# Turning the gated FFN chunks with VectorE blocks and strided stores instead of TensorE transposes

## The chip, the core and the metric

The kernel runs on one core of a Trainium2 chip. The core has a matrix engine (TensorE, PE in the profile, with its weight loads as PEld), a vector engine (VectorE, DVE), a scalar engine (ScalarE, ACT), GpSimd (POOL) and a queue that issues DMA transfers (SyncE, SP). The engines run side by side, each with its own instructions in a fixed order, and wait for each other by semaphores. DMA transfers are moved by 16 DMA engines. The metric is the time of one execution on the device in microseconds.

## The reference: what is computed

One decoder layer on 512 tokens of width 2048, in float32. The part around the change is the last line, the gated feed-forward network (FFN) with 5632 hidden columns:

```python
mix = jnp.concatenate([out_a.astype(x.dtype), out_b.astype(x.dtype)], axis=-1)
x = x + mix @ w_out[l]
h2 = rms_norm(x, norm2_g[l])
x = x + (jax.nn.silu(h2 @ w_gate[l]) * (h2 @ w_up[l])) @ w_down[l]
```

Before it come the input projection, a gated linear attention on four heads and a dilated attention on eight heads, which the change does not touch.

## The kernel before

**Products.** A float32 product is made from single-pass products of rounded parts: an operand is split into a rounded high part and the rest. ACT makes the high part of a weight tile (`wh`, line 376) and DVE the low part (`wl`, line 380). On top of that the kernel multiplies matrices with Strassen's scheme in Winograd's form: each product of 2x2 blocks takes seven block products P1 to P7 in place of eight. For them DVE adds and subtracts weight tiles (line 298).

**Pairs and steps.** The work goes over "pairs" of 512 output columns. An FFN pair j (there are 11, 0 to 10) multiplies the normed tokens with 512 columns of `w_gate` and the same 512 of `w_up`. Its seven products take the order P1, P5, P6, P3, P7, P2, P4, each over four groups of rows: 28 steps of twelve 128x512 matmuls (line 405), eight with `wh` and four with `wl`. A step needs one `wh` and one `wl`; two buffers of each exist. The weight tiles of a pair are called a, b, d and c in the order in which they are loaded, four of each, 512 KB per tile, and twelve buffers hold them. P5 uses b - a, P7 d - b, P6 d - a and P4 c - a (`wa<-wb,wa` and so on at line 298).

**The gated chunk.** When both the gate and the up columns of a half of the tokens (256 of 512, two tiles `m` of 128) are done, `final_ffn` takes Silu on ACT and multiplies on DVE (line 1396). The result is a tile of 128 tokens by 512 hidden columns. The down projection needs it with the hidden columns on the partitions. So `transposed_store` (line 1092) turns it: eight 128x128 transposes on PE into two PSUM banks, two copies by ACT into the tiles `oT` and `PT` (line 1107), and two stores of 256 KB to DRAM (`p_d`, line 1116). The first half of a pair does this in the middle of step 26 of its pair, the second half in step 2 of the next pair.

**What reads it.** After the second half, `sums_job` loads four parts of the chunk (`r<-p_d`, line 1167), forms the sums S1 to S4 that the down projection will need on DVE (lines 1421 to 1428) and stores them (`S_d`, line 1416). During pair 10, `down_jobs` loads parts and sums for the first stage of the down projection and splits them (line 199).

**What sets the order.** The code of each step is written in one order, but a scheduler of the framework then places the instructions of each engine, and the DMA issues of SP, by its own estimate of when their inputs are there. Each engine and SP keep to the order so found: a waiting instruction holds up all behind it. The tile pool `mp` gives each of `oT` and `PT` one buffer, so a new tile waits until the store of the old one has landed. A DMA also waits until the eighth one before it has landed.

Of the kernel before, what the change touches and what calls it, by code (L numbers as in the profile page):

```python
# [18 lines left out]
P = 128  # L19
# [112 lines left out]
def block_kernel(ctx: ExitStack, tc: tile.TileContext, ins, out):  # L132
    nc = tc.nc
# [18 lines left out]
    def nm(s):  # L152
        uid[0] += 1
        return f"{s}_{uid[0]}"

    def dram(shape, name):
        return dr.tile(shape, F32, name=name, tag=name)

    def bank():
        return ps.tile([P, 512], F32, name=nm("bank"), tag="bank")  # L160

    def work(tag, shape=(P, 512), bufs=1):
        return mp.tile(list(shape), F32, name=nm(tag), tag=tag, bufs=bufs)
# [7 lines left out]
    store = nc.sync.dma_start  # L171
# [14 lines left out]
    done = set()  # L186


    class Operand:


        def __init__(self, groups):
            self.groups = groups
            self.t = {}
# [71 lines left out]
    def unfolded(t):  # L266

        return t.rearrange("p (a b) -> p b a", b=2)

    def halves(t):  # L270
        return t.rearrange("p (b a) -> p b a", b=2)
# [311 lines left out]
    def later(units, fn, hold=False):  # L583

        deferred.append([units, fn, hold])
# [506 lines left out]
    def transposed_store(tiles, half, dsts, gains=None, spare=None):  # L1092

        for b in range(2):
            bk = bank().rearrange("p (j n) -> p j n", j=2)
            for jj in range(2):
                for m in range(2):
                    f = (2 * b + jj) * P
                    nc.tensor.transpose(  # L1099
                        bk[:, jj, m * P : (m + 1) * P], tiles[m][:, f : f + P], ident  # L1100
                    )
            if spare is None:
                d = work(("oT", "PT")[b], (P, 2, 256))
            else:
                d = spare[b]
            if gains is None:
                nc.scalar.copy(d, bk)
            else:
                for jj in range(2):
                    nc.scalar.activation(  # L1110
                        d[:, jj, :], bk[:, jj, :], AF.Copy,
                        scale=gains[:, 2 * b + jj : 2 * b + jj + 1],
                    )
            if dsts is None:
                continue
            store(dsts[b][half], d)
            done.add((id(dsts[b]), half))
# [255 lines left out]


    rows_n = [(512, 0), (768, 256), (1536, 1024), (1792, 1280)]
    p_d = [dram([2, P, 2, 256], f"p_d{b}") for b in range(22)]
    tok_scale = lambda half, m: rs2[:, 2 * half + m : 2 * half + m + 1]

    def final_ffn(j):
        ups = {}  # L1380

        def final(half, which, tiles, acc_):
            if which == 1:
                ups[half] = tiles
                return
            up = ups[half]
            for m in range(2):
                if tiles is None:
                    s = work(("q", "k")[m])
                    nc.scalar.activation(  # L1390
                        halves(s), unfolded(acc_[m]), AF.Silu, scale=tok_scale(half, m)
                    )
                else:
                    s = tiles[m]
                    nc.scalar.activation(s, s, AF.Silu)
                nc.vector.tensor_tensor(up[m], up[m], s, op=ALU.mult)
            def rest():
                transposed_store(up, half, p_d[2 * j : 2 * j + 2])
                if half == 1:
                    background.append(sums_job(j))  # L1400

            later(1 + (half == 1), rest)

        return final
# [4 lines left out]
    def sums_job(j):  # L1409

        top, bot = p_d[2 * j], p_d[2 * j + 1]
        tt = nc.vector.tensor_tensor
        s, t, u, v = part(bot, 1)(), part(top, 1)(), part(top, 0)(), part(bot, 0)()

        def put(name, src):
            store(sums_d[j][name][0], src)
            done.add((id(sums_d[j][name]), 0))

        yield
        yield  # L1420
        tt(s, t, s, op=ALU.add)
        put("S1", s)
        tt(t, u, t, op=ALU.subtract)
        put("S3", t)
        yield
        tt(u, s, u, op=ALU.subtract)
        put("S2", u)
        tt(v, v, u, op=ALU.subtract)
        put("S4", v)
        yield  # L1430
# [139 lines left out]
```

## Time and profile before

| what | value |
|---|---|
| time of three runs, median (lowest to highest) | 1930.76 us (1928.1 to 1931.49) |
| the profiled execution | 1928.26 us, span 1926.5 us |
| PE busy | 1915.5 us, 99% of the span |
| DVE busy | 1648.5 us, 86% |
| ACT busy | 1091.1 us, 57% |
| 128x128 transposes on PE, all (line 1099) | 248 |
| DMA packets | 150360, of which 15494 under 512 bytes |

In this profile a line of a group names the source line, the engine and the operation, then the tiles written and read and their shapes; the time in order names start and duration in microseconds, and in brackets how long the engine was idle before and what released it. "Busy" of PE counts pipelined matmuls whose ends are modelled. SPq is the queue that issues DMAs; its durations are those of the issue, not of the transfer. The granted clock of PE is 1.000 throughout.

### The profile page before, as it was taken

The page shows a single profiled execution, that of the slowest core. Times are in us where ns is not written, and L with a number is a line of the kernel's source. Part 1 is how long each engine was busy: PE and PEld are TensorE (multiplying, and loading weights), DVE is VectorE, ACT ScalarE, POOL GpSimd, SP SyncE. Part 2 cuts the span into 40 slices and gives each one's busy share as a digit, 9 for nine tenths or more (in the row PEclk, how much of TensorE's full clock was granted, in tenths as well). Part 3 has the DMA queues.
Part 4 walks back from the last instruction along what each step waited for, and adds up shares of the span by engine and source line. Part 5 has one row for each costly group of instructions (what it writes and reads, how often), then busy time and mean ns, then how long its engine had stood idle before and what let it go on. Part 6 is the DMA issues. An engine that isn't in the chain of part 4 may idle for free.

```text
span 1926.5 us, 25570 instructions
## 1 busy us (share of the span) xinstructions
PE 1915.5 (99%) x9178; PEld 1662.2 (86%) x9178; DVE 1648.5 (86%) x1912; ACT 1091.1 (57%) x1611; POOL 13.4 (1%) x22
## 2 busy tenths in 40 slices
PE   9999999999999999999999999999999999999999
PEld 7888888888888888888888888888888888888887
DVE  8898797778899998887877878878879989989987
ACT  8654564567776675554544544544546646546443
POOL 0000010000000000000000000000000000000000
PEclk9999999999999999999999999999999999999999
DMA  9536445444537454354355354454455865855762
GB/s 339 207 111 248 152 160 186 137 164 142 195 112 260 155 187 154 136 181 162 129 180 164 132 175 156 140 186 139 157 183 177 279 217 182 294 194 181 242 218 66
DMA packets 150360, 345.75 MB, mean 179 GB/s; under 512 B 15494, under 2 KB 42671, under 8 KB 150232
## 3 DMA queue, kind: packets, MB, share of 16 engines
q1 hardware_dynamic: 149944, 343.98, 53.2%
q8 instruction: 72, 1.18, 0.3%
q14 instruction: 56, 0.46, 0.1%
q10 hardware_dynamic: 288, 0.14, 0.0%
HBM read 286.10 MB, written 60.31 MB: 180 GB/s over the span
## 4 chain that ended last, share of the span: by engine, by line
PE 85%; DVE 5%; issue 2%; DMA 2%; ACT 1%; DVEq 0%; SPq 0%; ACTq 0%
PE acc L405 79%; DVE wl L380 2%; PE bank L1099 1%; PE bank L1003 1%; PE bank L979 1%; DVE wa L298 1%; DVE AS L199 1%; PE bank L996 0%; DMA xn_d<-oT 0%; PE bank L918 0%; DMA x_d<-seed 0%; PE bank L901 0%; DMA q<-y_d 0%; PE bank L970 0%; DVE AA L199 0%
## 5 line engine op out<-in xcount | busy, mean ns | idle before, releaser
L405 PE MATMUL acc<-wh,AS 128*128 128x512 f32 x3008 | 710.7, 379 | 0.0
L405 PEld LDWEIGHTS acc<-wh,AS 128*128 128x128 f32 x3008 | 568.4, 189 | 80.9 <-ACT wh L376 0.3
L376 ACT CAST wh<-wa 128x1024 fp32r<-128x1024 f32 x376 | 394.3, 1049 | 399.6 <-PE acc L405 370.8
L405 PE MATMUL acc<-wh,AA 128*128 128x512 f32 x2256 | 533.5, 379 | 0.1
L380 DVE TENSOR_TENSOR wl<-wa,wh 128x1024 fp32r<-128x1024 f32 x376 | 457.7, 1220 | 79.3 <-ACT wh L376 47.5
L405 PEld LDWEIGHTS acc<-wh,AA 128*128 128x128 f32 x2256 | 426.2, 189 | 60.7 <-ACT wh L376 0.3
L405 PE MATMUL acc<-wl,AS 128*128 128x512 f32 x1504 | 393.8, 384 | 1.1 <-DVE wl L380 0.9
L405 PEld LDWEIGHTS acc<-wl,AS 128*128 128x128 f32 x1504 | 279.7, 189 | 50.6 <-DVE wl L380 9.5
L405 PE MATMUL acc<-wl,AA 128*128 128x512 f32 x1128 | 296.6, 385 | 0.3
L405 PEld LDWEIGHTS acc<-wl,AA 128*128 128x128 f32 x1128 | 209.7, 189 | 32.2 <-DVE wl L380 2.7
L376 ACT CAST wh<-wb 128x1024 fp32r<-128x1024 f32 x94 | 98.6, 1049 | 123.9 <-PE acc L405 120.2
L376 ACT CAST wh<-wc 128x1024 fp32r<-128x1024 f32 x94 | 98.5, 1048 | 118.4 <-PE acc L405 104.6
L376 ACT CAST wh<-wd 128x1024 fp32r<-128x1024 f32 x94 | 98.6, 1049 | 95.9 <-PE acc L405 90.3
L380 DVE TENSOR_TENSOR wl<-wc,wh 128x1024 fp32r<-128x1024 f32 x94 | 114.7, 1221 | 39.6 <-ACT wh L376 38.8
L298 DVE TENSOR_TENSOR wa<-wc,wa 128x1024 f32<-128x1024 f32 x94 | 114.5, 1222 | 35.6 <-DMA wc<-in_w_gate 22.5
L380 DVE TENSOR_TENSOR wl<-wd,wh 128x1024 fp32r<-128x1024 f32 x94 | 114.5, 1221 | 31.5 <-ACT wh L376 28.3
L380 DVE TENSOR_TENSOR wl<-wb,wh 128x1024 fp32r<-128x1024 f32 x94 | 114.3, 1219 | 10.0 <-ACT wh L376 8.5
L298 DVE TENSOR_TENSOR wb<-wd,wb 128x1024 f32<-128x1024 f32 x94 | 114.4, 1220 | 0.4
L298 DVE TENSOR_TENSOR wa<-wb,wa 128x1024 f32<-128x1024 f32 x94 | 113.8, 1221 | 0.8
L298 DVE TENSOR_TENSOR wa<-wd,wa 128x1024 f32<-128x1024 f32 x94 | 113.2, 1219 | 0.1
L343 DVE SCALAR_TENSOR_TENSOR seed<-acc,rs,seed 128x512 f32<-128x512 f32 x96 | 70.5, 746 | 22.0 <-PE acc L405 20.9
L324 ACT ACTIVATE seed<-acc,rs 128x512 f32<-128x512 f32 x96 | 60.7, 681 | 5.1 <-PE acc L405 5.1
(317 smaller groups left out, 1304.8 us busy)
## 6 DMA issues: line engine op xcount, KB each, us to landing
wa<-in_w_gate SPq DMA_DIRECT2D x44, 512.0 KB, 3.5
wb<-in_w_up SPq DMA_DIRECT2D x44, 512.0 KB, 4.3
wd<-in_w_up SPq DMA_DIRECT2D x44, 512.0 KB, 4.2
wc<-in_w_gate SPq DMA_DIRECT2D x44, 512.0 KB, 3.4
wa<-in_w_in SPq DMA_DIRECT2D x24, 512.0 KB, 5.2
wc<-in_w_in SPq DMA_DIRECT2D x24, 512.0 KB, 3.5
wb<-in_w_in SPq DMA_DIRECT2D x24, 512.0 KB, 4.9
wd<-in_w_in SPq DMA_DIRECT2D x24, 512.0 KB, 5.1
```

Of the source, the lines that this page charges most:

```text
L199: nc.vector.tensor_tensor(a[:, :, 1, :], src, a[:, :, 0, :].bitcast(F32), op=ALU.subtract)
L298: nc.vector.tensor_tensor(src, other, src, op=ALU.subtract)
L324: nc.scalar.activation(halves(t), unfolded(src[m]), AF.Copy, scale=self.scale(half, m))
L343: nc.vector.scalar_tensor_tensor(halves(seed[m]), unfolded(src[m]), self.scale(half, m), halves(seed[m]), op0=ALU.mult, op1=ALU.add,)
L376: nc.scalar.copy(high[k], sources[k])
L380: recent["low"] = nc.vector.tensor_tensor(low[k], sources.pop(k), high[k].bitcast(F32), op=ALU.subtract).ins
L405: nc.tensor.matmul(p.dst[prod][m], a[:, jj, hl, m * P : (m + 1) * P], folded(w[i][:, jj, :]), start=fresh and g == 0 and i == 0 and jj == ...
L979: nc.tensor.matmul(lp[:, :n], qh[:, b * P : (b + 1) * P], kh[:, :n], start=True, stop=True)
L1003: nc.tensor.matmul(op, vh[:, k, :], lgs[b][:, k * P : (k + 1) * P], start=(k == 0), stop=(k == b))
L1099: nc.tensor.transpose(bk[:, jj, m * P : (m + 1) * P], tiles[m][:, f : f + P], ident)
```

## The change

For the nine pairs 1 to 9 the chunk is no longer turned by PE. DVE turns each of the two tiles of a half in blocks of 32x32 within the tile (`STREAM_TRANSPOSE`, one instruction per tile of 128x512, into `oT` and `PT`). The blocks are then put into their places by the stores: four per tile, each from 32 partitions, 16 runs of 32 numbers per partition, so 512 pieces of 128 bytes per store (64 KB). The DRAM tensor of such a chunk is `turned_d`, in which one hidden column is a run of 256 tokens (1 KB); the later loads of the chunk read it through the class `Turned` in pieces of 1 KB instead of 2 KB. Pairs 0 and 10 keep the old way.

```diff
     rows_n = [(512, 0), (768, 256), (1536, 1024), (1792, 1280)]
-    p_d = [dram([2, P, 2, 256], f"p_d{b}") for b in range(22)]
+    turned_d = {j: dram([2, 4, P, 256], f"turned_d{j}") for j in range(1, 10)}
+
+    class Turned:
+
+        def __init__(self, j, b):
+            self.t, self.b = turned_d[j], b
+
+        def __getitem__(self, half):
+            return self.t[half, 2 * self.b : 2 * self.b + 2].rearrange("q p n -> p q n")
+
+    p_d = [
+        Turned(b // 2, b % 2) if b // 2 in turned_d else dram([2, P, 2, 256], f"p_d{b}")
+        for b in range(22)
+    ]
+
+    def turned_store(tiles, half, j):
+
+        dst = turned_d[j][half].rearrange("q (k i) n -> i (q k) n", i=32)
+        for m in range(2):
+            d = work(("oT", "PT")[m])
+            nc.vector.transpose(d, tiles[m])
+            for a in range(4):
+                store(
+                    dst[:, :, m * P + 32 * a : m * P + 32 * a + 32],
+                    d[32 * a : 32 * a + 32, :].rearrange("i (c n) -> i c n", n=32),
+                )
+        for b in range(2):
+            done.add((id(p_d[2 * j + b]), half))
+
     tok_scale = lambda half, m: rs2[:, 2 * half + m : 2 * half + m + 1]
...
             def rest():
-                transposed_store(up, half, p_d[2 * j : 2 * j + 2])
+                if j in turned_d:
+                    turned_store(up, half, j)
+                else:
+                    transposed_store(up, half, p_d[2 * j : 2 * j + 2])
                 if half == 1:
                     background.append(sums_job(j))
```

The scheduler answers to this with another order. The first place is DVE's queue for steps 4 to 7 of pair 2, in the kernel before; `wl` rows make the low parts, rows of line 298 the weight sums, and `r` rows the sums of the chunk.

```order
L380 TENSOR_TENSOR wl_7909<-wa_7767,wh_7904 128x1024
L298 TENSOR_TENSOR wb_7927<-wd_8015,wb_7927 128x1024
L380 TENSOR_TENSOR wl_7930<-wa_7801,wh_7925 128x1024
L298 TENSOR_TENSOR wa_7767<-wd_7977,wa_7767 128x1024
L298 TENSOR_TENSOR wa_7801<-wd_7996,wa_7801 128x1024
L1421 TENSOR_TENSOR r_7892<-r_7894,r_7892 128x512
L380 TENSOR_TENSOR wl_7955<-wa_7821,wh_7950 128x1024
L1423 TENSOR_TENSOR r_7894<-r_7896,r_7894 128x512
L380 TENSOR_TENSOR wl_7980<-wa_7845,wh_7975 128x1024
L1426 TENSOR_TENSOR r_7896<-r_7892,r_7896 128x512
L298 TENSOR_TENSOR wa_7821<-wd_8015,wa_7821 128x1024
L1428 TENSOR_TENSOR r_7898<-r_7898,r_7896 128x512
```

After the change DVE's queue there, from the `wl` of step 2 to that of step 6, holds the second half's two block transposes instead.

```order
L380 TENSOR_TENSOR wl_7834<-wa_7808,wh_7830 128x1024
L1396 STREAM_TRANSPOSE oT_7863<-seed_7441 128x512
L298 TENSOR_TENSOR wa_7788<-wb_7889,wa_7788 128x1024
L380 TENSOR_TENSOR wl_7853<-wa_7832,wh_7848 128x1024
L298 TENSOR_TENSOR wa_7808<-wb_7910,wa_7808 128x1024
L380 TENSOR_TENSOR wl_7892<-wa_7758,wh_7887 128x1024
L1396 STREAM_TRANSPOSE PT_7869<-seed_7462 128x512
L298 TENSOR_TENSOR wa_7832<-wb_7935,wa_7832 128x1024
L380 TENSOR_TENSOR wl_7913<-wa_7788,wh_7908 128x1024
L298 TENSOR_TENSOR wa_7758<-wd_7960,wa_7758 128x1024
L298 TENSOR_TENSOR wa_7788<-wd_7979,wa_7788 128x1024
L380 TENSOR_TENSOR wl_7938<-wa_7808,wh_7933 128x1024
```

The transposes are not next to each other: the second one stands two steps behind the first. The four sums on `r` have left this place; they stand at the `wl` of steps 10 to 13 now, behind the last weight sums.

```order
L380 TENSOR_TENSOR wl_8001<-wa_7788,wh_7996 128x1024
L298 TENSOR_TENSOR wa_7832<-wd_8019,wa_7832 128x1024
L380 TENSOR_TENSOR wl_8022<-wa_7808,wh_8017 128x1024
L298 TENSOR_TENSOR wb_7935<-wd_8019,wb_7935 128x1024
L1452 TENSOR_TENSOR r_7875<-r_7877,r_7875 128x512
L380 TENSOR_TENSOR wl_8040<-wa_7832,wh_8038 128x1024
L1454 TENSOR_TENSOR r_7877<-r_7879,r_7877 128x512
L1457 TENSOR_TENSOR r_7879<-r_7875,r_7879 128x512
L380 TENSOR_TENSOR wl_8056<-wd_7960,wh_8054 128x1024
L1459 TENSOR_TENSOR r_7881<-r_7881,r_7879 128x512
```

Here the weight sum on `wd_8019` (the fourth of the d tiles) stands ahead of the `wl` of step 10, and the first sum on `r` ahead of that of step 11.

The second place is SP's queue over the same change of pair. Before, the fourth d tile of pair 2 is loaded first, then the stores of the two halves of pair 1 follow, each pair of stores with the load of a part behind it, then the loads of `r`.

```order
L259 DMA wd_8036<-in_w_up 128x1024
L1116 DMA p_d_162<-oT_7784 128x512
L1116 DMA p_d_163<-PT_7792 128x512
L1197 DMA T_12600<-p_d_162 128x512
L1116 DMA p_d_162<-oT_7881 128x512
L1116 DMA p_d_163<-PT_7889 128x512
L1167 DMA r_7892<-p_d_163 128x512
L1167 DMA r_7894<-p_d_162 128x512
L1167 DMA r_7896<-p_d_162 128x512
L1167 DMA r_7898<-p_d_163 128x512
```

After it the 16 stores of the two halves stand together (x4 are four rows that read alike), and the load of the fourth d tile has moved behind all of them.

```order
L259 DMA wd_7998<-in_w_up 128x1024
L1398 DMA turned_d_160<-oT_7770 32x16x32 x4
L1398 DMA turned_d_160<-PT_7776 32x16x32 x4
L1398 DMA turned_d_160<-oT_7863 32x16x32 x4
L1398 DMA turned_d_160<-PT_7869 32x16x32 x4
L259 DMA wd_8019<-in_w_up 128x1024
L1197 DMA T_12519<-turned_d_160 128x2x256
L1167 DMA r_7875<-turned_d_160 128x2x256
L1167 DMA r_7877<-turned_d_160 128x2x256
L1167 DMA r_7879<-turned_d_160 128x2x256
```

The loads of `r` wait for all 16 stores, the load `wd_8019` for the buffer and for the store eight places ahead of it.

## The prediction

> **What bounds the kernel now.** I read the page's busy shares first, then the stretches of the FFN, then PE's order of time over one change of pair, and last what VectorE (DVE) and the DMA queue (SP) do in the same microseconds.
>
> ```profile
> PE 1915.5 (99%) x9178; PEld 1662.2 (86%) x9178; DVE 1648.5 (86%) x1912; ACT 1091.1 (57%) x1611; POOL 13.4 (1%) x22
> 848.00:923.00 75.00, 75.00 (x357) 65.62 (x356) 60.72 (x59) 37.53 (x43) 0.00 (x0) 1.00 0.49 163
> 1448.00:1523.00 75.00, 74.95 (x353) 64.82 (x352) 74.69 (x87) 51.32 (x70) 0.00 (x0) 1.00 0.74 248
> ```
>
> The columns of the last two are stretch, length, then busy time of PE, weight loads, DVE, ACT and POOL, granted clock (1.00), DMA share and GB/s. PE has no gap in an FFN pair; DVE has 14 us of slack in 75, and next to none in the last pair. So PE work taken away shows in the time, unless something else becomes late.
>
> ```profile
> 844.47 1.89 PE L405 MATMUL acc<-wh,AA 128*128 128x512 f32 x8
> 846.20 1.04 PE L1099 MATMUL bank<-mats,seed 128*128 128x128 f32 x8
> 846.99 1.11 PE L405 MATMUL acc<-wl,AA 128*128 128x512 f32 x4
> 847.94 1.89 PE L405 MATMUL acc<-wh,AA 128*128 128x512 f32 x8
> 849.66 1.03 PE L405 MATMUL acc<-wl,AA 128*128 128x512 f32 x4
> 850.53 1.89 PE L405 MATMUL acc<-wh,AA 128*128 128x512 f32 x8
> 857.43 1.04 PE L1099 MATMUL bank<-mats,seed 128*128 128x128 f32 x8
> 868.67 1.03 PE L405 MATMUL acc<-wl,AS 128*128 128x512 f32 x4
> 879.06 1.03 PE L405 MATMUL acc<-wl,AS 128*128 128x512 f32 x4
> ```
>
> One step of PE (8 matmuls with wh, 4 with wl) goes from 847.94 to 850.53, 2.59 us. With a half's eight transposes inside it lasts from 844.47 to 847.94, 3.47 us. A pair has 28 steps; I number those of the next pair from 0 (850.53). The transposes stand in step 26 of a pair (846.20) and in step 2 of the next (857.43). The row of 868.67 is the wl part of step 6, that of 879.06 of step 10.
>
> **PE: what goes.** Nine pairs with two halves are 18 groups of eight transposes, each worth 3.47 - 2.59 = 0.87 us on an engine that never waits: 18 x 0.87 = 15.7 us. The 36 PSUM copies go from ACT too, which is 57% busy: no gain counted.
>
> **DVE: what is added.** Two block transposes per half, 36 in all. No row shows one. The nearest is a DVE pass over the same 128x512 tile:
>
> ```profile
> L1396 DVE TENSOR_TENSOR seed<-seed,seed 128x512 f32<-128x512 f32 x22 | 15.0, 683 | 0.0
> 843.50 0.68 DVE L1396 TENSOR_TENSOR seed<-seed,seed 128x512 f32<-128x512 f32 x1
> 844.94 1.22 DVE L380 TENSOR_TENSOR wl<-wa,wh 128x1024 fp32r<-128x1024 f32 x1 [0.76 <-ACT wh L376]
> 848.20 1.23 DVE L380 TENSOR_TENSOR wl<-wa,wh 128x1024 fp32r<-128x1024 f32 x1 [2.03 <-PE acc L405]
> 852.99 0.69 DVE L1396 TENSOR_TENSOR seed<-seed,q 128x512 f32<-128x512 f32 x1
> 853.60 0.68 DVE L1396 TENSOR_TENSOR seed<-seed,k 128x512 f32<-128x512 f32 x1
> 859.87 1.22 DVE L298 TENSOR_TENSOR wa<-wb,wa 128x1024 f32<-128x1024 f32 x1
> 861.01 1.22 DVE L380 TENSOR_TENSOR wl<-wa,wh 128x1024 fp32r<-128x1024 f32 x1
> 867.29 1.22 DVE L380 TENSOR_TENSOR wl<-wa,wh 128x1024 fp32r<-128x1024 f32 x1
> 880.34 1.22 DVE L380 TENSOR_TENSOR wl<-wd,wh 128x1024 fp32r<-128x1024 f32 x1 [0.94 <-ACT wh L376]
> 846.40 1.05 ACT L376 CAST wh<-wa 128x1024 fp32r<-128x1024 f32 x1 [1.49 <-PE acc L405]
> ```
>
> From start to start such a pass costs 0.61 us (852.99 to 853.60), a 128x1024 pass 1.14 (859.87 to 861.01; 0.605 and 1.135 over longer runs). I take 0.61 for a block transpose, since it moves as many elements; the ends are half of it (0.3) and two such passes (1.3).
>
> *First half.* Its two transposes stand right behind the product of 843.50, where DVE sat idle for 0.76 and then 2.03 us. They fit (1.2 us): cost nothing.
>
> *Second half.* DVE has no gap from 848.20 to 879.4, and there it is as close to the bound as PE: the wl of step 6 ends at 867.29 + 1.22 = 868.51, and PE takes it at 868.67, a lead of 0.16 us. There PE will come 2 x 0.87 = 1.75 us earlier, at 866.92. So I add up DVE's queue by the order of the changed program. The run starts at 847.5 instead of 848.20, when the ACT cast of 846.40 is through (PE frees the buffer earlier). Before, up to that wl: 16 passes of 1.135 and 3 of 0.605, 20.0 us, ending at 868.27 with the last one's tail; the trace has 0.24 more, which I carry along. After: 14 large (7 wl, 7 weight sums) and 4 small (2 products, 2 transposes), 18.3 us, since the two later weight sums and the first sum on r stand further back: end 847.5 + 18.3 + 0.1 + 0.24 = 866.1. Lead 0.8 us; transposes hidden, no stall. By the same count T2, the second transpose, starts at 859.8, the first weight sum that reads wd's fourth tile at 872.9 (it holds back the wl of step 10, with a lead of 2.1 us), and the first sum on r at 876.3.
>
> **SP and the DMA engines: what is added.** 36 stores become 144, each of 512 pieces of 128 bytes; a half is eight stores. Now:
>
> ```profile
> 859.19 0.32 SPq L1116 DMA_DIRECT2D p_d<-oT  x1
> 859.68 0.32 SPq L1116 DMA_DIRECT2D p_d<-PT  x1
> 861.91 1.74 SPq L1167 DMA_DIRECT2D r<-p_d  x4
> 867.40 5.53 SPq L1416 DMA_DIRECT2D S_d<-r  x4
> 881.59 8.92 SPq L259 DMA_DIRECT2D wc<-in_w_gate  x4
> 117.11 0.37 SPq L840 DMA_DIRECT2D q<-qa  x1
> L792 SPq DMA_DIRECT2D kT<-k x4: 577/585/636, 90.7 to 92.6; - x4
> S_d<-r SPq DMA_DIRECT2D x44, 256.0 KB, 2.0
> 118.00:119.50 1.50, 1.50 (x8) 1.16 (x7) 1.50 (x2) 1.47 (x3) 0.00 (x0) 1.00 0.59 180
> 860.00:861.50 1.50, 1.50 (x8) 1.31 (x8) 1.50 (x2) 0.40 (x1) 0.00 (x0) 1.00 0.93 350
> 863.00:866.50 3.50, 3.50 (x18) 3.06 (x17) 3.50 (x4) 1.58 (x3) 0.00 (x0) 1.00 0.91 291
> ```
>
> The stretch from 860.00 holds the two p_d stores, 256 pieces of 2 KB: 0.93 x 1.50 x 16 engines / 256 = 87 ns a piece. That from 118.00 holds the load q, 512 pieces of 512 bytes (117.11): 0.59 x 1.50 x 16 / 512 = 28 ns. The line through both gives 13 ns for 128 bytes, so 32 pieces per engine last 0.4 us. Let p be the time of one new store in a row of them. Low end: 0.4 us (an SP issue takes 0.32 to 0.58, the latter for a 32-row tile). High end: 1.5 us, all the time that the 512 larger pieces took alone. I take 1.0, nearest to the 0.9 us of engine time of that load. No store of pieces under 1 KB is in the trace; that is the weak point.
>
> When does p hurt? A first-half store is issued at 844.8; data starts 1.0 us later (861.91 to 863.00) and lands 0.3 us after its end (S_d: 2.0 = 1.0 + 0.7 + 0.3). So the first half has landed at 846.1 + 8p, both at 846.1 + 16p, or for small p at 861.8 + 4p. Three things wait:
> - T2 overwrites PT, still being stored: 846.1 + 8p must be under 859.8 plus the lead of 0.8, so p under 1.8.
> - wd's fourth load now stands behind all 16 stores and shares their engines: it lands some 2.0 us after them, needed by 872.9 + 2.1. So p under 1.68. This binds first.
> - r is read after all have landed, 3.3 us more (issue to two of four loads), needed at 876.3: p under 1.68 as well.
>
> At p = 1.0 the stores have landed at 865.8, wd's fourth tile is there at 867.8 and r at 869.1: nothing is late. Reads of turned_d come in 1 KB pieces, 47 ns by the line above: 0.75 us a tile for 0.70, in time that SP and the engines have free until about 880, when the wc loads start behind the S_d stores as before. Above 1.68 a pair loses 16p - 26.9 us; against the 1.75 gained, p = 1.79 decides the sign.
>
> **The last pair.** The second half of pair 9 falls into pair 10, where DVE is busy 74.69 of 75. Lost at worst: 0.87 + 1.22 = 2.1 us; at best nothing, since three sums on r move back there too. Nearer the latter: 0.5.
>
> **Sum.** The profiled execution took 1928.26 us (span 1926.5 and 1.8 around it): 1928.26 - 15.7 + 0.5 = 1913.1. The median of the runs is 2.5 us above that execution, so 1930.76 - 15.2 = 1915.5.
>
> The Trainium skill, page "DMA: Bandwidth & Descriptors", section "Specifications", says that under 512 bytes a transfer misses line rate because of a read-modify-write. No run here shows it. It speaks against this change; the first rival is what it would do. "VectorE: DVE Perf Modes", section "The three transpose paths", warns that a plain DMA that transposes by strides is 19 times slower than the hardware one; by 19 times the two stores' 1.4 us, p would be 3.3 and the time about 2150. The pieces here are contiguous, so I give that no chance of its own.
>
> **Rivals.**
> 1. *Each piece is handled twice.* Two times the 28 ns of a 512-byte piece: p = 1.77, a loss of 1.5 us per pair at wd's fourth tile and r, 9 x (1.75 - 1.5) = 2 us gained: about 1928, and 14 us more or less for each 0.1 us of p.
> 2. *The stores are slow (other side).* From p = 1.79 the DVE queue stands at T2 and at wd's fourth tile until the stores land, and PE behind it. p = 2.0 gives 5.1 - 1.75 = 3.4 us per pair: 1961; p = 2.5 gives 11.4 per pair: 2033. For it: no small store in the trace, and SP reads r only after the last has landed. Against it: 28 ns at 512 bytes.
> 3. *DVE becomes the bound.* A transpose of 1.3 us eats 1.4 of a lead of 0.8: 0.6 us per pair, 1921. At 2.4 us it is 2.8 per pair: 1940. For it: the gapless 31 us; against it: the moved sums.
>
> **Chances.** My forecast 0.59, its own range 1912 to 1920; rival 1 0.10 (0.04 faster, 0.02 same, 0.04 slower); rival 2 0.18; rival 3 0.13 (0.07, 0.02, 0.04). A measurement tells this kernel from no change by about 0.2%, 3.9 us. Faster 0.59 + 0.11 = 0.70, same 0.04, slower 0.26. The range 1911 to 1970 leaves out p above 2.1 and a little below, under 0.2.
>
> **What would show it.** Right: no L1099 rows between 800 and 1490 us, pairs 72.6 us apart instead of 74.3, PE without gaps, block transposes of 0.6 to 0.7 us, turned_d stores of about 1 us each in the DMA share, r landed before DVE asks. Wrong: DVE idle before L1396 or L298 released by a DMA of turned_d or wd, and PE steps over 2.59 us near steps 4 to 11.

## The result, and the profile after

The changed kernel takes 1919.51 us (median of four runs, 1917.44 to 1922.53) beside 1931.12 us for the kernel before in the same session: a ratio of 0.9944, 95% interval 0.9925 to 0.9963. It is faster, and 4 us short of the 1915.5 forecast. The page of the profiled execution (1921.12 us, span 1919.3) has these rows:

```profile
PE 1902.6 (99%) x9034; PEld 1648.3 (86%) x9034; DVE 1668.0 (87%) x1948; ACT 1073.2 (56%) x1575; POOL 13.1 (1%) x22
DMA packets 229271, 345.75 MB, mean 180 GB/s; under 512 B 90950, under 2 KB 134255, under 8 KB 229144
```

PE is still "99% busy", so the share cannot say where 4 us went. What can is the time at which PE begins the same step in both traces. Each fence has four rows from PE's order of time: step 14 of pair 0, then step 0 of pair 10, of the first and of the second pair of the down projection. The fence of the changed kernel also has step 0 of pair 2 (853.30), which the prediction shows for the kernel before (850.53). Before:

```profile
738.99 1.24 PE L405 MATMUL acc<-wh,AS 128*128 128x512 f32 x5
1445.00 1.24 PE L405 MATMUL acc<-wh,AA 128*128 128x512 f32 x5
1520.02 1.24 PE L405 MATMUL acc<-wh,AA 128*128 128x512 f32 x5
1593.46 1.03 PE L405 MATMUL acc<-wh,AA 128*128 128x512 f32 x4
```

After:

```profile
742.65 1.03 PE L405 MATMUL acc<-wh,AS 128*128 128x512 f32 x4
853.30 1.24 PE L405 MATMUL acc<-wh,AA 128*128 128x512 f32 x5
1435.71 1.03 PE L405 MATMUL acc<-wh,AA 128*128 128x512 f32 x4
1512.12 1.24 PE L405 MATMUL acc<-wh,AA 128*128 128x512 f32 x5
1586.47 1.24 PE L405 MATMUL acc<-wh,AA 128*128 128x512 f32 x5
```

- *Before the change's first instruction* the changed kernel is 742.65 - 738.99 = 3.66 us late. That is scatter, as a second profile of the same kernel shows below. So all gains from here on are counted from step 14 of pair 0.
- *To the start of pair 2:* one group of transposes fewer (step 26 of pair 1). 110.65 in place of 111.54 us: 0.89 gained.
- *Pairs 2 to 9:* 16 groups. 582.41 in place of 594.47 us: 12.1 gained, of 16 x 0.88 = 14.1. **Lost: 2.0.**
- *Pair 10:* one group. 76.41 in place of 75.02 us: 1.4 slower in place of 0.9 gained. **Lost: 2.3.** The first pair of the down projection is 0.9 slower too.
- *The rest* is alike within 0.2. Together 10.8 us gained.

In the 590 us of pairs 2 to 9, DVE's groups show what is late. Before, then after (tiles and shapes, times, busy us and mean ns, idle us ahead of them and what ended it):

```profile
L298 DVE TENSOR_TENSOR wa<-wc,wa 128x1024 f32<-128x1024 f32 x32 | 39.2, 1224 | 20.7 <-DMA wc<-in_w_gate 20.4
```

```profile
L298 DVE TENSOR_TENSOR wa<-wc,wa 128x1024 f32<-128x1024 f32 x32 | 39.2, 1225 | 28.8 <-DMA wc<-in_w_gate 28.1
L1396 DVE STREAM_TRANSPOSE oT<-seed 128x512 f32<-128x512 f32 x17 | 12.0, 704 | 0.0
L1396 DVE STREAM_TRANSPOSE PT<-seed 128x512 f32<-128x512 f32 x16 | 11.0, 687 | 0.0
```

The block transposes last 0.69 to 0.70 us and wait for nothing: no store of `oT` or `PT` is late. But the weight sums c - a stand 8 us more for the loads of the c tiles. Pair 2 in the order of time, after:

```profile
858.26 0.70 DVE L1396 STREAM_TRANSPOSE oT<-seed 128x512 f32<-128x512 f32 x1
858.99 1.93 SPq L1398 DMA_DIRECT2D turned_d<-oT  x4
866.15 0.44 SPq L259 DMA_DIRECT2D wd<-in_w_up  x1
867.52 1.91 SPq L1167 DMA_DIRECT2D r<-turned_d  x4
868.53 1.21 DVE L380 TENSOR_TENSOR wl<-wa,wh 128x1024 fp32r<-128x1024 f32 x1
870.57 1.03 PE L405 MATMUL acc<-wl,AS 128*128 128x512 f32 x4
876.48 1.21 DVE L298 TENSOR_TENSOR wa<-wd,wa 128x1024 f32<-128x1024 f32 x1
879.88 0.68 DVE L1452 TENSOR_TENSOR r<-r,r 128x512 f32<-128x512 f32 x1
880.59 2.79 SPq L1447 DMA_DIRECT2D S_d<-r  x3
882.95 1.22 DVE L380 TENSOR_TENSOR wl<-wd,wh 128x1024 fp32r<-128x1024 f32 x1
884.19 0.33 SPq L259 DMA_DIRECT2D wc<-in_w_gate  x1
888.28 1.23 DVE L298 TENSOR_TENSOR wa<-wc,wa 128x1024 f32<-128x1024 f32 x1 [2.26 <-DMA wc<-in_w_gate]
895.03 1.22 DVE L380 TENSOR_TENSOR wl<-wb,wh 128x1024 fp32r<-128x1024 f32 x1
896.47 1.03 PE L405 MATMUL acc<-wl,AS 128*128 128x512 f32 x4
```

and the end of the same chain before:

```profile
885.01 1.22 DVE L298 TENSOR_TENSOR wa<-wc,wa 128x1024 f32<-128x1024 f32 x1 [0.85 <-DMA wc<-in_w_gate]
892.01 1.22 DVE L380 TENSOR_TENSOR wl<-wb,wh 128x1024 fp32r<-128x1024 f32 x1
894.60 1.03 PE L405 MATMUL acc<-wl,AS 128*128 128x512 f32 x4
```

At step 6 the `wl` is done 870.57 - 869.74 = 0.8 us before PE takes it, what the prediction worked out. At step 16 the lead fell from 894.60 - 893.23 = 1.37 us to 896.47 - 896.25 = 0.22 us. The first c load goes out when the `wl` of step 12 is done: 882.95 + 1.22 = 884.17, issue at 884.19 (before: 880.34 + 1.22 = 881.56, issue at 881.59, rows of the prediction). Against PE's take at step 16 that is 12.28 us ahead now, 13.01 before. It also lands later, right behind three `S_d` stores: the sum that waits for it starts 888.28 - 884.19 = 4.1 us after the issue, before 885.01 - 881.59 = 3.4. With a lead of 0.2 us each slower load shows on PE.

Read in the same way in the other pairs from 2 to 9, the lead at step 16 is 0.1 to 0.4 us in all eight after the change; before it was 1.3 to 1.4 us in six, 0.6 in pair 7 and only 0.1 in pair 3. The loss is not spread evenly either: from its start to the start of the next a pair takes 72.5 to 72.6 us in the changed kernel, but 73.5 us in pair 3 and 73.1 in pairs 5 and 9. In pair 3 a c load took 4.65 us from issue to landing, and PE stood at step 16:

```profile
970.00 1.13 PE L405 MATMUL acc<-wl,AS 128*128 128x512 f32 x4 [0.75 <-DVE wl L380]
1468.96 0.62 ACT L198 CAST AS<-T 128x512 fp32r<-128x512 f32 x1 [3.77 <-DMA T<-S_d]
1471.28 2.00 PE L405 MATMUL acc<-wh,AS 128*128 128x512 f32 x8 [1.74 <-ACT wh L376]
```

The last two rows are pair 10, step 13: the load of a sum is late, ACT's split of it (line 198) waits, the next `wh` stands behind it, and PE idles 1.74 us.

### The profile page after: what moved, and what is told of

It is laid out like the page before. It is cut to its first block, busy times and chain, and to the rows that moved or that the text cites. A ratio compares the mean times of both kernels' runs of the same rounds, so it can differ in the third digit from the quotient of the medians.

```text
span 1919.3 us, 25358 instructions
## 1 busy us (share of the span) xinstructions
PE 1902.6 (99%) x9034; PEld 1648.3 (86%) x9034; DVE 1668.0 (87%) x1948; ACT 1073.2 (56%) x1575; POOL 13.1 (1%) x22
## 4 chain that ended last, share of the span: by engine, by line
PE 78%; DVE 8%; DMA 4%; issue 3%; ACT 0%; SPq 0%; DVEq 0%; ACTq 0%
PE acc L405 73%; DVE wl L380 4%; DVE wa L298 1%; PE bank L1003 1%; PE bank L979 1%; DMA wc<-in_w_gate 1%; PE bank L1099 0%; PE bank L996 0%; DMA wd<-in_w_out 0%; DVE AA L199 0%; DMA xn_d<-oT 0%; DVE AS L199 0%; DMA k<-x_d 0%; PE bank L918 0%; DMA k<-y_d 0%
## 5 line engine op out<-in xcount | busy, mean ns | idle before, releaser
L380 DVE TENSOR_TENSOR wl<-wd,wh 128x1024 fp32r<-128x1024 f32 x94 | 114.2, 1218 | 13.5 <-ACT wh L376 10.2
```

Source lines behind the costliest of these rows:

```text
L380: recent["low"] = nc.vector.tensor_tensor(low[k], sources.pop(k), high[k].bitcast(F32), op=ALU.subtract).ins
```

## The experiments

Three causes were open for the loss in pairs 2 to 9: the order (the sums on `r` moved back, so that their stores meet the c loads), the 128-byte pieces, or the time of the transposes on DVE. The table has all kernels; gains are read as above, from step 14 of pair 0 of each profiled execution. "Lost" is what pairs 2 to 9 gained less than 0.88 us for each group taken off PE there. "To the end" also holds what follows the first pair of the down projection; there the two profiles of the changed kernel differ by 0.8 us, so totals within about 1 us of each other are not told apart.

| kernel | median us | ratio to before (95%) | pairs 2-9 | lost there | pair 10 | down, 1st pair | to the end |
|---|---|---|---|---|---|---|---|
| changed | 1919.51 | 0.9944 (0.9925-0.9963) | 12.1 | 2.0 | -1.4 | -0.9 | 10.8 |
| e1 again | 1919.08 | 0.9943 (0.9928-0.9958) | 10.7 | 3.4 | -0.4 | -0.9 | 9.7 |
| e2 pairs 1 to 8 | 1917.44 | 0.9932 (0.9915-0.9948) | 10.8 | 2.4 | 0.0 | 0.0 | 11.9 |
| e3 whole stores | 1918.43 | 0.9939 (0.9924-0.9954) | 10.3 | 3.8 | 0.3 | -0.9 | 9.2 |
| e4 and late sums | 1920.0 | 0.9946 (0.9931-0.9961) | 9.0 | 5.1 | 0.2 | -0.9 | 8.7 |
| e5 no turning | 1914.35 | 0.9922 (0.9907-0.9937) | 13.8 | 0.3 | 0.6 | 0.0 | 14.3 |
| e6 turn twice | 1932.9 | 1.0014 (1.0005-1.0024) | -2.7 | 16.8 | -1.2 | -1.6 | -5.9 |
| e7 sums behind lows | 1917.92 | 0.994 (0.9925-0.9955) | 13.9 | 0.2 | -1.8 | -2.0 | 10.4 |
| e8 and pairs 1 to 8 | 1915.38 | 0.9925 (0.991-0.994) | 13.4 | none | -0.3 | -0.4 | 13.1 |
| e9 small, no turning | 1913.47 | 0.9914 (0.9899-0.9929) | 14.1 | none | 0.6 | -0.3 | 14.8 |
| e10 stores twice | 1984.78 | 1.0285 (1.027-1.0301) | -48.0 | 62 | -7.5 | -0.1 | -56.3 |
| e11 before, lows | 1930.22 | 0.9998 (0.9989-1.0008) | 0.1 | - | -0.3 | -1.4 | -1.5 |
| e12 lows, pairs 0 to 8 | 1914.28 | 0.992 (0.9905-0.9934) | 12.8 | 0.4 | -0.3 | 0.0 | 15.0 |

Two slips in the first expectation: the times 817.04 and 813.39 are those of step 14 of pair 1 (at pair 0 they are 742.65 and 738.99, the same distance), and the gaps that it puts at the start of pairs 4 and 6 are at step 16 of pairs 3 and 5. Some expectations also count a gain only up to the second pair of the down projection: 10.6 for the changed kernel, 10.2 for e1 and 11.7 for e2 are 10.8, 9.7 and 11.9 in the table.

**e1: the same again.** No edit.

> The changed kernel once more, nothing edited. In the first look at it PE began step 14 of pair 0, ahead of anything that the change touches, at 817.04 us against 813.39 in the kernel before, and gained 10.6 us from there to the end. Theory (chance upstream): this place moves by up to 3.7 us from run to run, 813.4 to 817.1, while the gain behind it repeats within 0.3 us (10.3 to 10.9), with the same gaps of PE at the start of pair 4, pair 6 and in the middle of pair 10. Rival (the build delays the stages ahead of the FFN): 817.0 again within 0.2 us.

Step 14 of pair 0 begins at 739.37 us, 0.4 us behind the kernel before; in the other runs it lies between 737.96 and 740.33. So the 3.7 us ahead of the change are scatter. Behind that place the gain is 9.7, less than the 10.3 to 10.9 expected: the gaps at step 16 of pairs 3 and 5 and in pair 10 are there again, with further ones in pairs 7 and 9 (1406.91). The loss repeats, its size does not: 2.0 and 3.4 us in pairs 2 to 9.

**e2: pair 9 as before.**

```diff
-    turned_d = {j: dram([2, 4, P, 256], f"turned_d{j}") for j in range(1, 10)}
+    turned_d = {j: dram([2, 4, P, 256], f"turned_d{j}") for j in range(1, 9)}
```

> Pair 9 goes back to the transposes on PE. Theory (pair 10 is the place of the loss): PE lost 2.3 us in pair 10 and 0.95 in the first steps of the down projection, because there the sums on pair 9's chunk moved behind ten more low parts; without it these 3.2 us come back and two groups of transposes (2 x 0.89) return: 1.4 us faster than the changed kernel, measured from step 14 of pair 0 to the end (12.0 gained in place of 10.6). Rival (the groups are independent and pair 10 loses for another reason): 1.8 us slower than the changed kernel (8.8 gained).

11.9, as the theory had it (12.0). Pair 10 and the first pair of the down projection cost what they cost before the change. So the turning of pair 9's chunk is what costs there, and it costs more than its two groups bring.

**e3: whole stores.**

```diff
             nc.vector.transpose(d, tiles[m])
-            for a in range(4):
-                store(
-                    dst[:, :, m * P + 32 * a : m * P + 32 * a + 32],
-                    d[32 * a : 32 * a + 32, :].rearrange("i (c n) -> i c n", n=32),
-                )
+            store(dst[:, 2 * m : 2 * m + 2], d.rearrange("p (q n) -> p q n", q=2))
```

Here `dst` is `turned_d[j][half]` seen as `p q n`.

> The block transposes stay on DVE, but each turned tile is stored whole, 256 KB in pieces of 1 KB, so that the blocks are not put into their places (this part of the computation is left out). The scheduler then puts the sums on r back to their old place, five low parts earlier, in pairs 2 to 9; in pair 10 they stay late. Theory (late sums): the 2.1 us that PE lost between pairs 2 and 9 come back, pair 10 still loses 3.2: 12.7 gained from step 14 of pair 0 to the end. Rival 1 (DVE's transposes are what made the low parts late): the loss stays, 10.6. Rival 2 (the 128-byte pieces cost the DMA engines time everywhere): more than 13 gained, pair 10 too.

My theory of the late sums fell. The sums are early again and no piece is small, yet 3.8 us are lost in pairs 2 to 9, and the whole gain is 9.2, below even rival 1. What is left is DVE: four early sums, 2.4 us, stand ahead of the `wl` of step 12 now, in place of three.

**e4: whole stores, late sums.** `sums_job` yields five times more for pairs 1 to 8, and the first two sums are queued behind the low part made last:

```diff
         yield
         yield
-        tt(s, t, s, op=ALU.add)
+        for _ in range(5 if 1 <= j < 9 else 0):
+            yield
+        with ExitStack() as behind:
+            if 1 <= j < 9:
+                behind.enter_context(tc.issue_after(recent["low"]))
+            tt(s, t, s, op=ALU.add)
...
```

> As the run with whole stores (the placing of the blocks is left out), but for the chunks of pairs 1 to 8 the sums on r are held back on DVE to the place that they have in the changed kernel. Theory (late sums, through their stores that meet the loads of the c tiles): the loss of about 2 us between pairs 2 and 9 is there again although no piece is smaller than 1 KB: 10.3 to 11.0 gained. Rival (small pieces): as with whole stores, 12.5 or more.

9.0 gained in pairs 2 to 9 against 10.3 in e3. The two executions differ by 1.3 us, and e1's scatter is as large (12.1 and 10.7), so that this alone settles nothing. It does not explain e3's own loss.

**e5: no turning at all.** As e3, and

```diff
-            d = work(("oT", "PT")[m])
-            nc.vector.transpose(d, tiles[m])
-            store(dst[:, 2 * m : 2 * m + 2], d.rearrange("p (q n) -> p q n", q=2))
+            store(dst[:, 2 * m : 2 * m + 2], halves(tiles[m]))
```

> As the run with whole stores, and the block transposes go too: the gated tiles are stored as they are, 256 KB in pieces of 1 KB (the turning of the chunk is left out altogether). It shows what the removal from PE alone is worth. Theory (VectorE's queue): between its wl of step 0 and step 12 DVE has no gap, so the two transposes of the second half, 1.2 us, make the wl of steps 12 to 15 late, with them the buffers of the d tiles, the loads of the c tiles into these, and at steps 16 to 20 PE. Without the transposes PE loses under 0.5 us between the start of pair 2 and that of pair 10 (3.4 and 3.9 with them), and about 1 us less in pair 10: 14.0 to 15.5 gained from step 14 of pair 0 to the end. Rival (loads of the c tiles are slow by themselves now and then, and a faster PE shows it): 3 to 4 us are lost again, 10 to 11.5 gained.

This is the new theory's first success: 14.3 gained, 0.3 lost in pairs 2 to 9. The group of c - a over pairs 2 to 9, and pair 2 in the order of time:

```profile
L298 DVE TENSOR_TENSOR wa<-wc,wa 128x1024 f32<-128x1024 f32 x32 | 39.2, 1225 | 19.5 <-DMA wc<-in_w_gate 19.4
```

```profile
877.78 1.23 DVE L380 TENSOR_TENSOR wl<-wd,wh 128x1024 fp32r<-128x1024 f32 x1
879.03 8.70 SPq L259 DMA_DIRECT2D wc<-in_w_gate  x4
882.32 1.23 DVE L298 TENSOR_TENSOR wa<-wc,wa 128x1024 f32<-128x1024 f32 x1 [0.76 <-DMA wc<-in_w_gate]
889.18 1.22 DVE L380 TENSOR_TENSOR wl<-wb,wh 128x1024 fp32r<-128x1024 f32 x1
892.01 1.03 PE L405 MATMUL acc<-wl,AS 128*128 128x512 f32 x4
```

The first c load goes out 892.01 - 879.03 = 12.98 us ahead of PE's take at step 16, as before the change (13.01), and the lead there is 1.61 us. Beside the changed kernel it is 1.39 us more, with two transposes fewer on DVE (some 0.62 us each from start to start) and one sum on `r` more ahead of the `wl` of step 12. What is still lost is lost in pair 5 alone, which takes 73.1 us where the others take 72.5. Its first c load took 4.4 us from issue to landing; in the other pairs whose landing the trace shows it took 3.1 to 3.6. In e7 and e9 the first c load of pair 5 is the slow one too (4.8 and 4.4 us). So the slow loads are not all chance; why that one is slow stays open.

**e6: turn twice.**

```diff
             nc.vector.transpose(d, tiles[m])
+            nc.vector.transpose(d, tiles[m])
```

> Each block transpose is done twice (the same tile again), all else as in the changed kernel. Theory (VectorE's queue): the second half puts 1.2 us more ahead of the wl of step 12 in each of nine pairs, the lead left at steps 16 to 20 is 0.2 us or so, hence about 1 us more lost per pair: 8 to 10 us slower than the changed kernel (0 to 2 gained from step 14 of pair 0 to the end). Rival (slow loads by themselves): within 2 us of the changed kernel, 8 to 11 gained.

The direction is the theory's, the size is larger: 5.9 us are lost in all, where 0 to 2 gained were expected. Put down to the second half's further two transposes, 1.24 us, it is (16.8 - 2.0) / 8 = 1.85 us per pair (1.7 against e1), not 1. PE now waits for low parts in every pair from 2 to 9, at step 14 and in most of them once more at step 16:

```profile
DVE wa L298 <- DMA wc<-in_w_gate: 36.2, 25, 3.0
PE acc L405 <- DVE wl L380: 13.6, 22, 2.0
```

(waits: total us, times, longest us; in the changed kernel the second row is 3.5 us, 7 times.)

**e7: the d - b sums behind the low parts.** The same transposes and stores; only the place of four sums on DVE moves, with `lows` a list of all low parts made so far:

```diff
                 if self.hold and "head" in recent:
                     behind.enter_context(tc.issue_after(recent["head"]))
+                if prod == "P7" and self.rows is rows_n:
+                    behind.enter_context(tc.issue_after(lows[-4]))
                 nc.vector.tensor_tensor(src, other, src, op=ALU.subtract)
```

> The changed kernel, and the weight sums d - b of an FFN pair are held back on DVE, so that only one of the four stands ahead of the wl of step 12 in place of all four (one more ahead of each later wl). Theory (VectorE's queue delays the release of the d tiles' buffers): the loads of the c tiles start up to 3 us earlier against PE, the sums c - a no longer wait 2 us, and of the 3.4 us that PE lost between the start of pair 2 and that of pair 10 under 0.7 are left: 12.5 to 14 gained from step 14 of pair 0 to the end, against 10.2 and 10.6 for the changed kernel. Rival 1 (slow loads): unchanged, 10 to 11. Rival 2 (the d - b sums are then late themselves): slower than the changed kernel, under 9 gained.

0.2 lost in pairs 2 to 9, as expected; the whole gain of 10.4 is below the 12.5 to 14 expected. How the first comes about is not as expected either:

```profile
L300 DVE TENSOR_TENSOR wa<-wc,wa 128x1024 f32<-128x1024 f32 x32 | 39.1, 1222 | 1.7 <-DMA wc<-in_w_gate 1.4
```

```profile
879.68 1.22 DVE L382 TENSOR_TENSOR wl<-wd,wh 128x1024 fp32r<-128x1024 f32 x1
880.81 1.22 DVE L300 TENSOR_TENSOR wb<-wd,wb 128x1024 f32<-128x1024 f32 x1
880.92 8.33 SPq L259 DMA_DIRECT2D wc<-in_w_gate  x4
884.27 1.23 DVE L300 TENSOR_TENSOR wa<-wc,wa 128x1024 f32<-128x1024 f32 x1
889.95 1.22 DVE L382 TENSOR_TENSOR wl<-wb,wh 128x1024 fp32r<-128x1024 f32 x1
893.00 1.03 PE L408 MATMUL acc<-wl,AS 128*128 128x512 f32 x4
```

The c load does not start earlier against PE (12.08 us ahead of the take at step 16). But DVE now does d - b sums while the load is under way, and no longer stands: 1.7 us of idle in all in place of 28.8, and a lead of 1.83 us. The whole gain is no larger because pair 10 and the pair behind it are 3.7 us slower than before the change. The scheduler's order there is new once more; which wait costs the time was not followed.

**e8: both.** e7 and e2's range of pairs.

> As the run before it, and pair 9 keeps the transposes on PE, as in the run with pairs 1 to 8, which gained 11.7. Theory: PE gains nearly the whole of its 16 groups, 14.0, loses under 0.7 in the pairs and nothing in pair 10: 13 to 14 gained, the fastest kernel so far, about 1916 us by the median. Rival (slow loads): 11.7 as without the edit of the sums.

13.1: nothing lost in pairs 2 to 9, 0.3 in pair 10 and 0.4 in the first pair of the down projection.

**e9: small stores, no turning.** As the changed kernel, with `d = tiles[m]` and no transposes.

> The gated tiles are stored in pieces of 128 bytes as in the changed kernel, eight stores of 64 KB per half, but without the block transposes (the turning is left out). It differs from the run without turning only in the pieces and in where the scheduler then puts the sums on r, four low parts later. Theory (VectorE's queue alone): the small stores cost nothing, 13.5 to 15 gained from step 14 of pair 0 to the end, as without turning (14.3), apart from up to 1 us in pair 10. Rival (the small pieces and the late sums cost time beside DVE): 10 to 12.5 gained.

14.8, as much as with large pieces (14.3). The eight stores of a half, their 128-byte pieces and the later sums on `r` cost nothing that shows as long as DVE has its lead. What the pieces take is seen in the changed kernel, in a stretch that has four stores (issued at 858.99) and no other transfer; the last two columns are the DMA share and GB/s:

```profile
859.90:861.90 2.00, 2.00 (x11) 1.76 (x10) 2.00 (x3) 1.05 (x1) 0.00 (x0) 1.00 0.75 128
```

128 GB/s for 2.00 us are 256,000 bytes, 2000 of the four stores' 2048 pieces. 0.75 x 2.00 us x 16 engines / 2000 = 12 ns a piece.

**e10: stores twice.**

```diff
-            for a in range(4):
+            for a in [0, 1, 2, 3] * 2:
                 store(
```

> Each of the 144 new stores is issued twice, to the same place; the block transposes are as in the changed kernel. The second transpose of a half moves five low parts back in DVE's order. In the changed kernel four stores take SP 1.9 to 2.1 us, 0.5 us a store, so a half's now last 8 us. Theory (a store costs 0.5 us, and the bound of 1.68 us for it is far): 16p rises from 8 to 16 us, no wait on the stores shows: 8 to 11 gained from step 14 of pair 0 to the end. Rival (the stores are already near a bound, by the tiles oT and PT or by wd): 2 us or more lost per pair, slower than the kernel before.

A plain miss: 55 us slower than before. The rows of pair 4:

```profile
1031.81 0.71 DVE L1396 STREAM_TRANSPOSE PT<-seed 128x512 f32<-128x512 f32 x1
1032.55 4.41 SPq L1398 DMA_DIRECT2D turned_d<-PT  x8
1037.01 0.50 SPq L259 DMA_DIRECT2D wd<-in_w_up  x1
1040.87 1.22 DVE L298 TENSOR_TENSOR wa<-wd,wa 128x1024 f32<-128x1024 f32 x1 [6.69 <-DMA wd<-in_w_up]
1043.30 3.61 PE L405 MATMUL acc<-wh,AS 128*128 128x512 f32 x8 [5.42 <-ACT wh L376]
```

From the first transpose (1019.87) to the issue of the fourth d tile's load 17.1 us go by, in the changed kernel 7.9 (858.26 to 866.15). Of the 9.2 us more, the stores' own time is 2.5 (eight take SP 4.4 us, four 1.9). The rest is order: the scheduler put the second transpose 12 us behind the first, not 5, and the load stands on SP behind the stores that follow it. DVE stands 6.7 us at d - a. I had seen the transpose move back and had not asked what on SP stands behind it. In this order the fourth d tile is the place where late stores hurt.

**e11: the kernel before, with e7's edit.**

> The kernel before the change (all transposes on PE) with the d - b sums held back as in the run with the sums behind the low parts. Theory: PE has no gap in an FFN pair of the kernel before, so there is nothing to win: 0 gained, within 0.6 us, from step 14 of pair 0 to the end of pair 9; the edit pays only where DVE's queue has become late. Rival (the edit helps by itself): 2 us or more gained.

0.1 us in pairs 2 to 9, a ratio of 0.9998. So in these pairs the edit wins nothing by itself; it gives back what the turning on DVE took. The 1.4 us that the first pair of the down projection loses here was not followed.

**e12: pairs 0 to 8, sums behind the low parts.** e8 with `range(0, 9)`.

> The fastest run so far (pairs 1 to 8, sums behind the low parts, 13.0 gained), with pair 0 turned by DVE too. Theory (a pair's two groups are worth 1.77 us wherever DVE's lead allows it, and pair 1 then runs as pair 2 did): 14.5 to 15 gained from step 14 of pair 0 to the end, about 1914 us by the median. Rival (pair 0 loads the stores of the attention's last parts and the first sums at the same time): no more than 13.0.

15.0 by the profiled execution, 1914.28 us by the median: 5 us below the changed kernel, and the lowest median here of a version that does the whole computation. The ranges of e12 (1913.66 to 1916.03) and e8 (1914.37 to 1915.77) overlap.

## Why the prediction came out right, and where it was off

- *PE, 18 groups at 0.87 us:* right. The first gave 0.89; with nothing put in their place (e9) PE kept 14.8 of 15.7.
- *Block transposes at 0.61 us:* right, 0.69 to 0.70 long and some 0.62 from start to start; rival 3's 1.3 us is out. The first half's two were hidden, as worked out: DVE still idled 0.98 us behind them in pair 1 (before the `wl` at 851.13).
- *Stores, p = 1.0 us:* too high, and without effect. Four stores take SP 1.93 us (858.99), 0.48 each. A piece took 12 ns, where the line through 2 KB and 512 bytes gave 13. Rivals 1 and 2 are out (rival 1's loss per pair is 1.4 by its own formula, not 1.5: 3 us gained in place of 2). `r` was loaded at 867.52 and wanted at 879.88, the fourth d tile loaded at 866.15 and wanted at 876.48. The formula 16p - 26.9 held the places of the transposes fixed; e10 shows that they are not.
- *DVE, second half:* the lead of 0.8 us at step 6 came out to a tenth. The step that failed is the conclusion drawn from it: **"Lead 0.8 us; transposes hidden, no stall."** I added up DVE's queue to step 10 and took the c loads "as before". They hang on the `wl` of step 12, which hangs on that queue, and PE comes 1.75 us earlier. The lead at step 16 shrank to 0.2 us, and c loads that take longer in some pairs, above all 3 and 5, did the rest: 2.0 and 3.4 us in two profiles. That is rival 3, DVE as the bound, at another place and at half of its transpose time; its price, 0.6 us per pair, was too high for it. e5, e6 and e7 show it from three sides: no transposes, twice the transposes, DVE's waits filled.
- *The last pair, 0.5 us, at worst 2.1:* mis-sized. Pair 10 and the pair behind it lost 3.2 us (2.3 and 0.9) in the first profile, 2.2 in e1, and nothing without pair 9 (e2). In pair 10 a late load held ACT (1468.96) in the one trace shown; which wait leads when is not settled, since e7 loses 4.6 there in another order.
- *Sum:* 15.2 forecast; less some 2.7 lost in the pairs and 2.2 more than allowed in the last pair leaves 10.3. The two profiles gained 10.8 and 9.7, the medians 11.2 to 11.6. The term of PE and the direction came out for the reason given. That the median fell inside the forecast's own range of 1912 to 1920, by 0.5 us, is in part luck: one loss was not foreseen and the other was allowed for at 0.5 us, and together they used up nearly all of the 4.5 us between the forecast and the end of the range.

## What to carry to other kernels

When work moves from the bounding engine to one that runs close behind, follow the second engine's lead through the whole period, up to the loads that its own instructions release: the lead is thinnest where a load, a sum and a low part stand in one row. An idle wait in the middle of such a queue can be filled with work that is not yet urgent, which here won back nearly all of the loss in pairs 2 to 9 (e7, e8). And this edit paid less at the seam between two stages than in the middle: leaving pair 9 out made the kernel faster (e2 beside the changed kernel, e8 beside e7).

## What the hardware showed beyond that

A long stall cost PE more than its length. In e10 PE idles 5.42 us, and the eight matmuls behind it take 3.61 us in place of 1.89; the granted clock of that kernel in stretches of 2 us there:

```profile
1042.00:1044.00 2.00, 0.70 (x2) 0.61 (x3) 1.95 (x3) 1.80 (x2) 0.00 (x0) 0.80 0.98 335
1044.00:1046.00 2.00, 2.00 (x6) 1.57 (x5) 2.00 (x3) 0.19 (x1) 0.00 (x0) 0.50 0.07 24
1046.00:1048.00 2.00, 2.00 (x9) 1.73 (x8) 1.93 (x4) 1.05 (x2) 0.00 (x0) 0.85 0.69 228
1048.00:1050.00 2.00, 2.00 (x11) 1.73 (x11) 1.43 (x2) 1.62 (x3) 0.00 (x0) 1.00 0.93 298
```

The clock (third number from the end) is 0.50 after the pause and 1.00 again some 4 us later, so the stall costs 5.4 + 1.7 = 7.1 us. The Trainium skill, page "TensorE: Matmul & The Clock Gate", Part 1, says that the array falls to half rate after an idle window of about 3.4 us; this trace agrees, with 0.50 after 5.42 us. The pauses of 0.75 and 1.74 us in the changed kernel left the matmuls behind them nearly as fast: four took 1.13 us in place of 1.03, eight 2.00 in place of 1.89. No pause near 3.4 us is shown here.

Small pieces were cheap in this case: a store's piece of 128 bytes took 12 ns of a DMA engine, a load's piece of 512 bytes 28 ns. The prediction quoted the page "DMA: Bandwidth & Descriptors" of the Trainium skill, section "Specifications", that transfers under 512 bytes miss line rate because of a read-modify-write. The trace agrees that the rate is missed: 12 ns for 128 bytes are 11 bytes per ns, beside 18 at 512 bytes and 24 at 2 KB (87 ns). But there is no step below 512 bytes from SBUF to DRAM: the piece stayed under the 13 ns of the line through the two larger ones. Whether a read-modify-write takes place, no run here shows.
